# Gate and up with three pairs of seven products in the second chunk, the residual stream put away by GpSimd in halves, and both token tiles' activations transposed in one step

## The chip, the core and the metric

The kernel runs on one core of a Trainium2 chip. Five engines work side by side, each through its own queue in order: TensorE (PE, matmuls; weights are loaded in a second row, PEld), VectorE (DVE), ScalarE (ACT), GpSimd (POOL) and SyncE (SP), which here only issues transfers (DMAs). Semaphores tie the queues together. The metric is the device time of one execution in microseconds (us), the median of some runs. The profile comes from one execution of its own.

## The reference

A trunk of two layers over 256 tokens of width 2048, all in float32. Each layer, shortened:

```python
h = rms_norm(x, pre_mix_norm[l])
m = hybrid_mixer(h, ...)              # w_in, two kinds of attention, w_o
x = x + rms_norm(m, post_mix_norm[l])
h = rms_norm(x, pre_ffn_norm[l])
f = (silu(h @ w_gate[l]) * (h @ w_up[l])) @ w_down[l]     # 2048 -> 5632 -> 2048
x = x + rms_norm(f, post_ffn_norm[l])
```

The change lies in the second half of a layer, and in how x is kept while it runs.

## The kernel before

**Tokens and products.** The tokens form two tiles (t) of 128. A float32 product is made of three matmuls of a reduced type: each operand is split into `hi` (rounded) and `lo` (what is left), and hi·hi, hi·lo and lo·hi are added up in PSUM (`product`, L921 to L927). For the weights ACT makes `hi` (L250) and DVE `lo` (L252), 128 × 1024 at a time, which is one *block*: 256 rows of a weight matrix by 512 columns. `raw134` is the 134th block in the order in which all weights are loaded; `hi134` and `lo134` are its parts.

**Gate and up.** The 5632 columns are worked in 11 chunks (c) of 512, each over 8 row pairs (kp) of 256. For one kp a block of gate and one of up are needed, for both token tiles. `eight` (L1035) makes that of 8 products, 24 matmuls. `seven` (L1045) makes it of 7 products, 21 matmuls, in the manner of Strassen, which needs more of the other engines. The block of up is loaded into a tile `T`, and the first half of the block of gate is added to it by a DMA that accumulates, issued by POOL (L211). The block of gate is loaded into a tile `G`. `mixed_weights` (L216 to L238) then makes further sums and their splits: six DVE operations instead of two, four on ACT instead of two. Sums over the tokens' side (`pair_sums` L1028 and `token_sums`, the tiles `f`, `s`, `sh`, `sl`) are formed once for each kp of a layer and used by every chunk. The seven products of all such kp of a chunk share four extra banks (`p1`, `p6`, `p7`, `q5`), which `shared_part` (L959 to L966) puts together into four tiles `w` when the last is done; only then can the next use of those banks begin.

Which kp are sevens stands in constants: in chunk 0, `FIRST_SEVEN` = (4, 6), in the order `FIRST_ORDER`; in every other chunk `SEVEN` = (2, 4, 5, 6). `FORM_AT` says ahead of which step n of chunk 0 the sums of a kp are formed: 4 and 6 at steps 1 and 2, 5 at step 4, 2 at step 5.

**The stream of weights.** `weight_order` fixes one order for all blocks. `fetch` (L184) issues the loads on SP in this order, except that a `T` is asked for up to four blocks early (`EARLY`, L186 to L188). There are 4 rooms for `raw`, 6 each for `hi` and `lo`, 3 for `G` and 4 for `T`; a load waits until its room is free, that is until `hi` and `lo` of the block four `raw` earlier are made, and all loads behind it on SP wait too. `feed` (L240) issues the splits. Blocks 134 to 143 are the first of gate and up in layer 0 that matter here: 134 to 137 and 142, 143 are plain, 138 (`G`) and 139 (`T`) belong to kp 4, 140 and 141 to kp 6.

**The order of work.** The program is written as one sequence, and a planner arranges the operations of each engine, partly under `high_priority` and `manual_schedule`. Each engine's order is fixed before the kernel runs. Where an operation is issued thus decides what it may stand behind.

**x.** The residual stream x lies in four tiles `x_t_h` (token tile t, half h of 1024 columns). Two stretches of each layer have no room for it, so it is written to DRAM and loaded back: `put_away`, called after the end of the output projection (L1007) and, between the layers, after that of the down projection (L1196). The write goes out in four DMAs of 512 KB from ACT's queue (L295), as soon as `rescale` (L480 to L492), which adds the branch to x in four steps of 512 columns, and the sums of squares (`inv_rms`, L407) are issued. `rescale` takes a function `then`, called after each of the four steps: so `transposed` (L375) turns x for the next product, into the tiles `xF` (for gate and up) or `xI` (for the next layer's input projection). `transposed` is four PE transposes, four ACT copies (L383) and four DVE operations (L388). In the first stage of gate and up `G140` lies where a tile of x lay.

**The turning of activations.** At the end of a chunk silu(gate)·up is formed for both token tiles, `sg[0]` and `sg[1]`. The generator `flip` (L1084 to L1090) transposes them on PE, four transposes to a token tile, with one ACT copy (L1089) each. It is started `DEFER_ACT` = 7 ticks into the next chunk; a tick is a place between products, and each `yield 1` puts the rest off to the next.

```python
def flip(sg=sg, at=at, c=c):
    for t in range(NT):
        pb = (bank if c % 2 else acc_bank)(f"actT_ps{l}_{c}_{t}")
        for j in range(4):
            nc.tensor.transpose(pb[:, j * P : (j + 1) * P], sg[t][:, j * P : (j + 1) * P], ident)
        nc.scalar.copy(at[:, :, t * P : (t + 1) * P], pb.rearrange("p (k q) -> p k q", k=4))
        yield 1
```

Of the kernel before, what the change touches and what calls it, by code (L numbers as in the profile page):

```python
# [9 lines left out]
F32 = mybir.dt.float32  # L10
# [7 lines left out]
P = 128  # L18
# [21 lines left out]
SEVEN = (2, 4, 5, 6)  # L40
FIRST_SEVEN = (4, 6)
FIRST_ORDER = (0, 1, 3, 2, 7, 4, 6, 5)
FORM_AT = {1: 4, 2: 6, 4: 5, 5: 2}
DOWN_SEVEN = (3, 6, 9, 12, 15, 18)

WARM = 13
# [4 lines left out]

def lambda_init(layer):
    return 0.8 - 0.6 * math.exp(-0.3 * layer)


def weight_order():

    order = []

    def queue_pair(name, l, kp, c):  # L60
        order.append((name, l, kp, c))
        return len(order) - 1

    plan = []
    sevens, plain = set(), set()
    for l in range(L):
        lay = {"in": {}, "o": {}, "gate": {}, "up": {}, "down": {}}
        for n, (ca, cb) in enumerate(PAIRS):
            for kp in IN_ORDER if n else range(KT // 2):
                lay["in"][ca, kp] = queue_pair("w_in", l, kp, ca)  # L70
                lay["in"][cb, kp] = queue_pair("w_in", l, kp, cb)
                if kp in IN_NOW[n]:
                    plain.add(lay["in"][cb, kp])
        order_o = [(c, kp) for kp in KP_O for c in (0, 1)]
        order_o += [(c, kp) for c in (2, 3) for kp in range(KT // 2)]
        lay["order_o"] = order_o
        for c, kp in order_o:
            lay["o"][c, kp] = queue_pair("w_o", l, kp, c)
        for c in range(FF // CW):
            for kp in FIRST_ORDER if c == 0 else range(KT // 2):  # L80
                lay["gate"][c, kp] = queue_pair("w_gate", l, kp, c)
                lay["up"][c, kp] = queue_pair("w_up", l, kp, c)
                if kp in (FIRST_SEVEN if c == 0 else SEVEN):
                    sevens.add(lay["up"][c, kp])
        for half in range(2):
            for kp in range(FF // P // 2):
                for c in (2 * half, 2 * half + 1):
                    lay["down"][c, kp] = queue_pair("w_down", l, kp, c)
                if kp in DOWN_SEVEN:
                    sevens.add(lay["down"][2 * half + 1, kp])  # L90
        plan.append(lay)
    return order, plan, sevens, plain
# [48 lines left out]
def kernel(  # L141
# [145 lines left out]
        cols = slice(h * D // 2, (h + 1) * D // 2)  # L287
        nc.sync.dma_start(xs[t][h], xv[t][:, cols] if src is None else src[:, t, cols])

    def put_away(nm):  # L290

        away.append(kept.tile([P, NT, D], F32, name=f"away_{nm}"))
        for t in range(NT):
            for h in range(2):
                nc.scalar.dma_start(away[-1][:, t, h * D // 2 : (h + 1) * D // 2], xs[t][h])  # L295

    x_pool = [None]

    def new_x_pool(nm):
        if x_pool[0] is not None:  # L300
            x_pool[0].release()
        x_pool[0] = tc.alloc_tile_pool(name=nm, bufs=1, side="right", reuse_waits="tile")
        return x_pool[0]
# [668 lines left out]
    for l in range(L):  # L972
# [29 lines left out]
        with tc.manual_schedule(engines={mybir.EngineType.Activation, mybir.EngineType.DVE}):  # L1002
            feed(idx + 6)
            for kp in range(4, 8):
                unit(accs, mix, idx + kp - 4, kp, (0,), False, kp == 7, 0)
            evac_chunk(pool, accs[0], mg, ssm, gpost, 3, 0, f"o{l}")
            rescale(mg, ssm, 0, f"o{l}")  # L1007
            for kp in range(4, 8):
                feed(idx + 3 + kp)
                fetch(min(idx + 8 + kp, idx + 12))  # L1010
                unit(accs, mix, idx + kp - 4, kp, (1,), False, kp == 7, 0)
                transposed(0, 32 + l * KT, xT, cols=(kp - 4,))
        with tc.high_priority(offset=URGENT):
            evac_chunk(pool, accs[1], mg, ssm, gpost, 3, 1, f"o{l}")
            rescale(mg, ssm, 1, f"o{l}", lambda t, c: transposed(t, 32 + l * KT, xT, cols=(c,)))
        rs = [inv_rms(t, pool, f"ffn{l}") for t in range(NT)]
        put_away(f"ffn{l}")
        pool.release()


# [30 lines left out]

        for c in range(FF // CW):
            banks = four_banks(c % 2, [f"c{q}_{l}_{c}" for q in ("11", "12", "21", "22")])
            mine = FIRST_SEVEN if c == 0 else SEVEN
            order = FIRST_ORDER if c == 0 else tuple(range(KT // 2))
            if c == 0:
                for t in range(NT):
                    for kp in order[:2]:
                        eight(banks, c, kp, (t,), kp == order[0], False)
                order = order[2:]  # L1060
            extra = None
            for n, kp in enumerate(order):
                if c == 0 and n in FORM_AT:
                    with after_rests():
                        pair_sums(FORM_AT[n])
                if kp not in mine:
                    eight(banks, c, kp, range(NT), kp == 0, kp == order[-1])
                    continue
                if kp == mine[0]:
                    extra = four_banks(1 - c % 2, [f"{q}_{l}_{c}" for q in ("p1", "p6", "p7", "q5")])  # L1070
                seven(banks, extra, c, kp, kp == mine[0], kp == mine[-1])
                if kp == mine[-1]:
                    w = [pool.tile([P, CW], F32, tag="t2", name=f"w{j}_{l}_{c}") for j in range(4)]
                    shared_part(extra, w)
            at = pool.tile([P, 4, S], F32, tag="act", bufs=FF // CW, name=f"act{l}_{c}")
            act.append(at)
            sg = [w[0], w[2]]
            for t, u in ((0, w[1]), (1, w[3])):
                nc.vector.tensor_tensor(out=sg[t], in0=banks[2 * t], in1=sg[t], op=shared_sign(t, 0))
                nc.scalar.activation(sg[t], sg[t], AF.Silu, scale=rs[t][:, 0:1])  # L1080
                nc.vector.tensor_tensor(out=u, in0=banks[2 * t + 1], in1=u, op=ALU.add)
                nc.vector.scalar_tensor_tensor(out=sg[t], in0=u, scalar=rs[t][:, 0:1], in1=sg[t], op0=ALU.mult, op1=ALU.mult)
# [4 lines that stand above are left out]
                    for j in range(4):  # L1087
                        nc.tensor.transpose(pb[:, j * P : (j + 1) * P], sg[t][:, j * P : (j + 1) * P], ident)
                    nc.scalar.copy(at[:, :, t * P : (t + 1) * P], pb.rearrange("p (k q) -> p k q", k=4))  # L1089
                    yield 1  # L1090

            start(flip(), DEFER_ACT)
        gu.release()
# [9 lines left out]
        for half in range(2):  # L1103
# [64 lines left out]
            if half == 1:  # L1168
                xT = None
                if l + 1 < L:  # L1170
                    new_x_pool(f"x{l + 1}")
                    xT = x_tiles(f"xI{l}")
            for t in range(NT):
                if not tail:
                    for c in cc:
                        evac_sum(pool, accs[c, t], mg, ssm, gpost, c, t, f"d{l}")
                    continue
                for c in cc:
                    for kp in range(nkp - tail, nkp):
                        tick()  # L1180
                        prep(kp)
                        jh, jl = split[kp]
                        hi, lo = weights(plan[l]["down"][c, kp], LOOKAHEAD)
                        for kk in range(2):
                            sh, sl = jh[:, kk, t * P : (t + 1) * P], jl[:, kk, t * P : (t + 1) * P]
                            last = kp == nkp - 1 and kk == 1
                            nc.tensor.matmul(accs[c, t], sh, hi[:, kk, :], start=False, stop=False)
                            nc.tensor.matmul(accs[c, t], sh, lo[:, kk, :], start=False, stop=False)
                            nc.tensor.matmul(accs[c, t], sl, hi[:, kk, :], start=False, stop=last)
                    with tc.high_priority(offset=URGENT):  # L1190
                        evac_sum(pool, accs[c, t], mg, ssm, gpost, c, t, f"d{l}")
                with tc.high_priority(offset=URGENT):
                    rescale(mg, ssm, t, f"d{l}", store if xT is None else lambda t, c: transposed(t, (l + 1) * KT, xT, cols=(c,)))
        if l + 1 < L:
            rs = [inv_rms(t, pool, f"in{l + 1}") for t in range(NT)]
            put_away(f"in{l + 1}")  # L1196
        if l + 1 == L:
            x_pool[0].release()
        dn.release()
# [51 lines left out]
```

## Time and profile before

| | |
|---|---|
| median of 3 runs | 2214.32 us (2211.67 to 2216.69) |
| the profiled execution | 2215.14 us, span 2213.4 us |
| granted TensorE clock | 0.998 of full |
| matmuls and transposes | 10009 |
| transfers | 466.73 MB, mean 211 GB/s |
| gate and up | about 407 to 880 us in layer 0, 1507 to 1980 us in layer 1 |

The span runs from the first to the last instruction; 1.74 us of the profiled execution lie outside it. A row of the timeline gives the start and the duration in us, the engine, the line, the operation, the tile written and those read, and in brackets how long the engine sat idle before it and what ended that. `SPq` and `ACTq` are the sequencers that issue transfers; a row with "x3" holds three instructions in a row, and its duration includes what the queue waited between them. In the view of waits each line gives a waiting line, what it waited for, the total in us, how many times, and the longest.

### The profile page before, as it was taken

The numbers are of one execution on the slowest core, as the hardware profiler recorded it, in microseconds if no ns is written. First come the engines' busy times: TensorE is split into PE (matmuls) and PEld (weight loads), VectorE is DVE, ScalarE is ACT, GpSimd is POOL, SyncE is SP. The second block draws the span as 40 slices with busy tenths as digits, with TensorE's granted clock in tenths as the row PEclk, the third lists the DMA queues.
The fourth block names the chain that finished last, engine by engine and source line by source line (L and its number), as shares of the span: only waits on it lengthen the run. The fifth ranks groups of instructions, "written<-read, shape, count | busy, mean of one in ns | idle before, by whom it ended". The sixth has DMA issues, their size and how long they took to land.

```text
span 2213.4 us, 28454 instructions
## 1 busy us (share of the span) xinstructions
PE 2185.5 (99%) x10009; PEld 1790.9 (81%) x10009; DVE 1864.0 (84%) x2548; ACT 1354.6 (61%) x2030; POOL 142.2 (6%) x184
## 2 busy tenths in 40 slices
PE   9999999999999999999999999999999999999998
PEld 7788888778888888888888888887788888888886
DVE  7888655899999998989788886559999999999897
ACT  7566664656656656656565656646666556566564
POOL 1200000000000000000011000000000000000000
PEclk9999999999999999999999999999999999999999
DMA  8654555776776775767465545558677677667672
GB/s 304 208 180 153 190 176 186 250 237 215 218 256 211 211 258 180 241 215 240 157 239 190 177 160 177 174 187 268 208 225 235 224 221 238 226 204 243 200 254 98
DMA packets 138079, 466.73 MB, mean 211 GB/s; under 512 B 15824, under 2 KB 16336, under 8 KB 137424
## 3 DMA queue, kind: packets, MB, share of 16 engines
q1 hardware_dynamic: 120512, 430.30, 56.3%
q0 software_dynamic: 15552, 28.32, 7.5%
q10 hardware_dynamic: 1872, 6.31, 0.7%
q8 instruction: 78, 1.28, 0.2%
q14 instruction: 65, 0.53, 0.1%
HBM read 456.47 MB, written 8.39 MB: 210 GB/s over the span
## 4 chain that ended last, share of the span: by engine, by line
PE 78%; DVE 11%; DMA 4%; issue 3%; ACT 3%; SPq 0%; DVEq 0%; ACTq 0%
PE c L925 7%; PE c L926 7%; PE c L927 7%; PE in L925 5%; PE in L927 5%; PE in L926 5%; PE dn L1136 5%; PE dn L1135 5%; PE dn L1138 5%; DVE lo L252 3%; DMA raw<-in_weights_in_turn_dram 3%; PE o L464 3%; PE o L466 3%; PE o L465 3%; DVE Tl L226 2%
## 5 line engine op out<-in xcount | busy, mean ns | idle before, releaser
L252 DVE TENSOR_TENSOR lo<-raw,hi 128x1024 fp32r<-128x1024 f32 x534 | 643.3, 1223 | 161.4 <-ACT hi L250 161.2
L250 ACT ACTIVATE hi<-raw 128x1024 fp32r<-128x1024 f32 x534 | 552.4, 1053 | 235.1 <-DMA raw<-in_weights_in_turn_dram 63.5
L925 PE MATMUL c<-hi,xF 128*128 128x512 f32 x820 | 321.8, 395 | 6.2 <-DVE w L966 4.0
L926 PE MATMUL c<-lo,xF 128*128 128x512 f32 x820 | 320.0, 391 | 0.0
L927 PE MATMUL c<-hi,xF 128*128 128x512 f32 x820 | 318.3, 390 | 0.0
L211 POOL DMA_DIRECT2D T<-in_weights_in_turn_dram x108 | 94.3, 873 | 1669.3 <-PE c L926 520.9
L925 PEld LDWEIGHTS c<-hi,xF 128*128 128x128 f32 x820 | 153.7, 188 | 40.8 <-DVE w L966 6.3
L1135 PE MATMUL dn<-hi,jh 128*128 128x512 f32 x464 | 180.7, 389 | 0.0
L1136 PE MATMUL dn<-lo,jh 128*128 128x512 f32 x464 | 180.5, 389 | 0.0
L926 PEld LDWEIGHTS c<-lo,xF 128*128 128x128 f32 x820 | 154.1, 188 | 32.0 <-DVE lo L252 1.6
L927 PEld LDWEIGHTS c<-hi,xF 128*128 128x128 f32 x820 | 153.9, 188 | 32.1
L252 DVE TENSOR_TENSOR lo<-G,hi 128x1024 fp32r<-128x1024 f32 x108 | 131.7, 1220 | 26.7 <-ACT hi L250 26.6
L225 ACT ACTIVATE Th<-T 128x512 fp32r<-128x512 f32 x108 | 67.8, 627 | 138.6 <-DVE T L232 126.7
L1138 PE MATMUL dn<-hi,jl 128*128 128x512 f32 x464 | 142.9, 389 | 0.0
L226 DVE TENSOR_TENSOR lo<-T,hi 128x1024 fp32r<-128x1024 f32 x108 | 131.7, 1220 | 10.9 <-ACT hi L225 10.3
L226 DVE TENSOR_TENSOR Tl<-G,Th 128x1024 fp32r<-128x1024 f32 x108 | 131.8, 1220 | 9.6 <-ACT Th L225 9.6
L225 ACT ACTIVATE hi<-T 128x1024 fp32r<-128x1024 f32 x108 | 113.4, 1050 | 40.4 <-PE c L927 19.9
L225 ACT ACTIVATE Th<-G 128x1024 fp32r<-128x1024 f32 x108 | 113.9, 1054 | 36.6 <-DVE G L233 35.2
L233 DVE TENSOR_TENSOR G<-G,T 128x1024 f32<-128x1024 f32 x108 | 132.0, 1222 | 2.1
L925 PE MATMUL in<-hi,xT 128*128 128x512 f32 x328 | 131.5, 402 | 0.5 <-ACT hi L738 0.5
L925 PE MATMUL in<-hi,xI 128*128 128x512 f32 x328 | 131.3, 402 | 0.2 <-ACT xI L383 0.2
L926 PE MATMUL in<-lo,xT 128*128 128x512 f32 x328 | 128.2, 391 | 1.0 <-DVE lo L252 0.8
(376 smaller groups left out, 4660.2 us busy)
## 6 DMA issues: line engine op xcount, KB each, us to landing
raw<-in_weights_in_turn_dram SPq DMA_DIRECT2D x534, 512.0 KB, 4.7
T<-in_weights_in_turn_dram SPq DMA_DIRECT2D x108, 512.0 KB, 4.7
G<-in_weights_in_turn_dram SPq DMA_DIRECT2D x108, 512.0 KB, 4.8
T<-in_weights_in_turn_dram POOLq DMA_DIRECT2D x108, 256.0 KB, 6.7
GU<-in_weights_in_turn_dram SPq DMA_DIRECT2D x32, 512.0 KB, 4.6
away_ffn<-x ACTq DMA_DIRECT2D x8, 512.0 KB, 6.1
xd<-away_ffn SPq DMA_DIRECT2D x8, 512.0 KB, 9.2
xr<-in_x_columns_dram SPq DMA_DIRECT2D x8, 256.0 KB, 6.7
```

The source lines that it names most:

```text
L211: nc.gpsimd.dma_start(sums[i][:, 0, :], stream[i - 1][:, 0, :], accum_op=ALU.add)
L225: nc.scalar.activation(h, w, AF.Copy)
L226: nc.vector.tensor_tensor(out=l, in0=w, in1=h.bitcast(F32), op=ALU.subtract)
L233: nc.vector.tensor_tensor(out=g, in0=g, in1=t2.unsqueeze(1).to_broadcast([P, 2, CW]), op=ALU.add)
L250: nc.scalar.activation(hi, raw, AF.Copy)
L252: rest = nc.vector.tensor_tensor(out=lo, in0=raw, in1=hi.bitcast(F32), op=ALU.subtract)
L925: nc.tensor.matmul(a, sh, hi, start=first, stop=False)
L926: nc.tensor.matmul(a, sh, lo, start=False, stop=False)
L927: nc.tensor.matmul(a, sl, hi, start=False, stop=last)
L1135: nc.tensor.matmul(accs[c, t], sh, hi[:, kk, :], start=first, stop=False)
L1136: nc.tensor.matmul(accs[c, t], sh, lo[:, kk, :], start=False, stop=False)
L1138: nc.tensor.matmul(accs[c, t], sl, hi[:, kk, :], start=False, stop=last)
```

## The change

Three parts, in one diff.

1. In chunk 1 the seven-product pairs are kp 4, 5 and 6; kp 2 is made of eight products there, and of seven from chunk 2 on. The token sums of kp 2 are formed ahead of step 3 of chunk 1 instead of step 5 of chunk 0.
2. x is put away by GpSimd. `put_away` is called from `rescale`'s `then`, and after every second step writes the half of x that is complete with a DMA from POOL's queue. The room in DRAM is made before (`room_away`).
3. `flip` turns both token tiles in one step: its `yield 1` stands after the loop.

```diff
+NEXT_SEVEN = (4, 5, 6)
-FORM_AT = {1: 4, 2: 6, 4: 5, 5: 2}
+FORM_AT = {(0, 1): 4, (0, 2): 6, (0, 5): 5, (1, 3): 2}
...
+def gate_sevens(c):
+
+    return (FIRST_SEVEN, NEXT_SEVEN)[c] if c < 2 else SEVEN
...
-                if kp in (FIRST_SEVEN if c == 0 else SEVEN):
+                if kp in gate_sevens(c):
...
-    def put_away(nm):
-
+    def room_away(nm):
         away.append(kept.tile([P, NT, D], F32, name=f"away_{nm}"))
-        for t in range(NT):
-            for h in range(2):
-                nc.scalar.dma_start(away[-1][:, t, h * D // 2 : (h + 1) * D // 2], xs[t][h])
+
+    def put_away(t, c):
+
+        if c % 2 == 1:
+            nc.gpsimd.dma_start(away[-1][:, t, (c - 1) * CW : (c + 1) * CW], xs[t][c // 2])
...
-            rescale(mg, ssm, 0, f"o{l}")
+            room_away(f"ffn{l}")
+            rescale(mg, ssm, 0, f"o{l}", put_away)
...
-            rescale(mg, ssm, 1, f"o{l}", lambda t, c: transposed(t, 32 + l * KT, xT, cols=(c,)))
+            rescale(mg, ssm, 1, f"o{l}", lambda t, c: (transposed(t, 32 + l * KT, xT, cols=(c,)), put_away(t, c)))
         rs = [inv_rms(t, pool, f"ffn{l}") for t in range(NT)]
-        put_away(f"ffn{l}")
...
-            mine = FIRST_SEVEN if c == 0 else SEVEN
+            mine = gate_sevens(c)
...
-                if c == 0 and n in FORM_AT:
+                if (c, n) in FORM_AT:
                     with after_rests():
-                        pair_sums(FORM_AT[n])
+                        pair_sums(FORM_AT[c, n])
...
                     nc.scalar.copy(at[:, :, t * P : (t + 1) * P], pb.rearrange("p (k q) -> p k q", k=4))
-                    yield 1
+                yield 1
...
+                    room_away(f"in{l + 1}")
                     xT = x_tiles(f"xI{l}")
...
-                    rescale(mg, ssm, t, f"d{l}", store if xT is None else lambda t, c: transposed(t, (l + 1) * KT, xT, cols=(c,)))
+                    rescale(mg, ssm, t, f"d{l}", store if xT is None else lambda t, c: (transposed(t, (l + 1) * KT, xT, cols=(c,)), put_away(t, c)))
         if l + 1 < L:
             rs = [inv_rms(t, pool, f"in{l + 1}") for t in range(NT)]
-            put_away(f"in{l + 1}")
```

Counted in the built programs: PE has 6 matmuls more, DVE 8 operations fewer, ACT 4 splits and 12 DMA issues fewer, POOL 12 DMA issues more and 2 accumulating ones fewer. On SP the number of loads is the same and their order differs in places: at the start of gate and up the loads of `raw142` and `raw143` come ahead of those of `T139`, `T141` and `G138`, behind which they stood before. On ACT `hi134` to `hi136` come ahead of `xF_12` to `xF_15`.

## The prediction

> **What bounds the kernel now.** First the page's busy rows, then what PE waits for, then the stretches around those waits. TensorE (PE) is the bound nearly everywhere.
>
> ```profile
> PE 2185.5 (99%) x10009; PEld 1790.9 (81%) x10009; DVE 1864.0 (84%) x2548; ACT 1354.6 (61%) x2030; POOL 142.2 (6%) x184
> ```
>
> A matmul row lasts 0.39 us, but the rows start 0.23 us apart (461.62, 461.85, 462.08): they are pipelined, and a matmul costs 0.227 us. What can be won without taking matmuls away is only what PE stands idle. The view of PE's waits lists it:
>
> ```profile
> PE c L925 <- DVE w L966: 4.0, 2, 2.1
> PE p L925 <- ACT Th L225: 2.0, 2, 1.0
> ...
> PE p L926 <- DVE Tl L226: 1.6, 4, 0.6
> PE c L925 <- ACT hi L250: 1.6, 4, 0.6
> ...
> PE q L925 <- ACT sh L937: 0.7, 2, 0.4
> ```
>
> The columns are total us, times, longest. Every one with an even count comes once or twice in each layer, at the start of gate and up, and at the same place. I measure each by how far the start of a matmul exceeds the 0.227 us of an undisturbed one; that adds about 0.11 to the wait shown. Layer 0, with layer 1 alike: (A) 407.8 to 420.3, `xF` and `hi`, 1.9, of which 1.36 are the two `hi` waits. (B) 439 to 443, `Tl` and `lo`, 0.9. (C) chunk 1's first pair of seven products, `sh` at 461.3 and `Th` at 465.8, 1.9. (D) 496.35, `w`, 2.3. (E) five of 0.3 to 0.95 between 508 and 613, 2.1. Later chunks have none: chunk to chunk 41.7 us (671.24 to 713.02 to 754.73), in which DVE is busy 39.1 of 41.8. So DVE has 2.7 us of slack in a steady chunk, and a delay at the start takes several chunks to work off: C, D and E are that.
>
> D, in the timeline of DVE and the chain of waits (start, duration, what):
>
> ```profile
> 490.44 0.68 DVE L964 TENSOR_TENSOR w<-p,w 128x512 f32<-128x512 f32 x1
> 493.87 1.23 DVE L252 TENSOR_TENSOR lo<-raw,hi 128x1024 fp32r<-128x1024 f32 x1 [2.74 <-ACT hi L250]
> 495.01 0.68 DVE L965 TENSOR_TENSOR w<-q,w 128x512 f32<-128x512 f32 x1
> 495.61 0.68 DVE L966 TENSOR_TENSOR w<-q,w 128x512 f32<-128x512 f32 x1
> ```
>
> ```profile
> 485.37 7.33 DMA raw<-in_weights_in_turn_dram
> ```
>
> A `lo` of a weight block whose load was only issued at 485.37 stands ahead of L965 and L966 on DVE, and PE needs the bank that L966 frees.
>
> The last thing to read is the first mixed block of gate and up, `T139`. It is loaded by SP, added to by POOL, and then split on ACT:
>
> ```profile
> 408.58 0.86 SPq L210 DMA_DIRECT2D T<-in_weights_in_turn_dram  x2
> 409.54 11.56 SPq L195 DMA_DIRECT2D G<-in_weights_in_turn_dram  x2
> 421.19 2.03 SPq L202 DMA_DIRECT2D raw<-in_weights_in_turn_dram  x3
> ```
>
> ```profile
> SPq L195 <- DMA away_ffn<-x: 10.7, 1, 10.7
> ```
>
> ```profile
> 414.22 1.01 POOL L211 DMA_DIRECT2D T<-in_weights_in_turn_dram  x1 [260.46 <-PE c L926]
> 416.75 0.87 POOL L211 DMA_DIRECT2D T<-in_weights_in_turn_dram  x1 [1.52 <-ACT xF L383]
> ```
>
> ```profile
> 413.35 1.14 ACT L383 ACTIVATE xF<-xT_ps,gains 128x128 fp32r<-128x128 f32 x4 [1.35 <-PE xT_ps L380]
> ...
> 418.30 3.89 ACT L250 ACTIVATE hi<-raw 128x1024 fp32r<-128x1024 f32 x4
> ...
> 427.26 1.04 ACT L225 ACTIVATE hi<-T 128x1024 fp32r<-128x1024 f32 x1
> ```
>
> SP loads `T139` at 408.58 (landed 413.56); POOL's addition goes out at 414.22 and lands 5.45 us later, at 419.67. ACT reads the block only at 427.26, so it has 7.6 us to spare. SP stands 10.7 us for x's write, since G140 lies where x lay. PE's first matmul with `Th139` is at 434.08.
>
> **The change, part by part.**
>
> Products. Each layer gets three more matmuls: 3 × 0.227 = +0.7 us. One pair of blocks fewer is mixed: DVE loses two operations of 1.14 and two of 0.60 us (pitches in the DVE timeline) = 3.5 us, ACT two, POOL one addition. DVE is not the bound in steady chunks, so the 3.5 us are worth only what they take from C, D and E. Chunk 1's first pair of seven is now kp 4 instead of kp 2: two more plain pairs stand before it (24 matmuls, 5.4 us each), against a lateness of 1.9. C goes: −1.9 (ends −1.9 and −1.0, if `sh` or `Th` of kp 4 is still late). D: in the changed program L965 and L966 stand ahead of that `lo`, behind the one before it, whose load may still be 0 to 1.5 us late: 0.5 is left, −1.8 (ends −2.3 and −0.8). E: five small waits for DVE, which now has 3.5 us less to do; I leave 0.7 of 2.1, −1.4 (ends −2.1 and 0). B stays at 0.9.
>
> x put away. Twelve 512 KB writes go from ACT's queue to POOL's. On ACT an issue lasts 0.33 us and lies beside other work: nothing. On POOL an issue lasts 0.87 to 1.01 us; the four of a place stand before the additions for `T139` and `T141`. The last half of x is ready at 414.4 by the row of before; POOL is free by 415.5, before the additions now come. SP no longer stands for 10.7 us. But the order of the queues moves with it, and this is the dear part: on SP the loads `raw142` and `raw143` (gate and up of kp 5) now stand *ahead* of `T139`, `T141`, `G138`. `raw143` takes `raw135`'s room and so waits for `lo135`. On ACT `hi134` to `hi136` move ahead of `xF_12` to `xF_15`: from 414.4, where `xF_11`'s row ends, at a pitch of 0.95, `hi135` ends at 416.4, and on DVE `lo134` and `lo135` (1.14 and 1.22, with a few small rows between) end near 418.0. So `T139` is issued at 418.4 instead of 408.58. It lands 4.98 us later (as before), 423.4; POOL issues at 423.5; the addition lands 5.45 us later in layer 0 (its row) and 6.8 in layer 1 (both rows there, 6.6 and 7.0): L = 429.0 and 430.3 on layer 0's clock, 429.7 on average. Ends: 428 (4.4 for the load, the least among the `T` rows of this stretch, and 5.0 for the addition) and 432 (the page's median of 6.7 for the addition, and 6.5 for a load behind others).
>
> From `hi139` to PE's first matmul with `Th139` ACT's queue takes 434.08 − 427.26 = 6.8, of which it idled 0.28: 6.5. That matmul comes at L + 6.5 = 436.2, against 434.08: **+2.1**. The 1.36 of `hi` waits in A do go, since `hi134` to `hi136` come earlier, but PE only reaches the wait for `Th139` so much sooner: nothing is left of it. DVE's `lo139`, 428.53 before, comes at L + 1.1 = 430.8, 2.3 late like PE, so B isn't changed.
>
> In the Trainium skill, "DMA: Bandwidth & Descriptors", section "Issuing engines are not separate DMA queues", transfers from all issuing engines share the same 16 DMA engines, so that another issuer saves only issue time. By it this part alone would be worth the ACT issues, 4 × 0.33 us a place, which lie beside other work: nothing. The row of SP's 10.7 us agrees: what counts there is where the write stands in order, not who carries it.
>
> Put-away between the layers: the four writes leave ACT, POOL is idle there, and a few `hi` move by under 1 us: 0 ± 1, in the sum once.
>
> Flip. Two groups of four transposes become one of eight. From PE's rows, a group of eight costs 0.88 (879.33 to 880.12 and the late start after it), one of four 0.44 each: a saving of about 0.02 in each of 20 chunks, −0.4. Both copies (L1089) then come together on ACT, which is at 61%.
>
> Sum per layer: +0.7 − 1.9 − 1.8 − 1.4 + 2.1 = −2.3. Two layers −4.6, flip −0.4: −5.0. The profiled execution took 2215.14 (span 2213.4 and 1.74 around it), 0.8 above the median of 2214.32. 2215.1 − 5.0 = 2210.1 on its clock, **2209** beside the median. With the ends of L alone (−1.7 and +2.3 in each layer) 2206 to 2214.
>
> **The rivals.** A change of under 0.2% (4.4 us) can hardly be told from none here.
>
> *T isn't late.* If `T139` lands by 427.3, say because `raw143`'s room is free earlier, the first matmul is no later, and A's 1.36 counts too: per layer +0.7 − 1.9 − 1.8 − 1.4 − 1.3 = −5.7, in all −11.8: 2203. For it: 7.6 us of slack before. Against: it needs 2.4 us less than the rows add up to.
>
> *The waits move one chunk on.* DVE's steady slack is 2.7 us a chunk and its sums for kp 2 are now formed inside chunk 1; the late load of D and the small waits of E return in chunk 2, where four pairs of seven begin again at kp 2. Then only C is won: +0.7 − 1.9 + 2.1 = +0.9 a layer, +1.8 − 0.4 in all: 2216. For it: E shows that a delay is carried through three chunks. Against: 3.5 us of DVE's work really go.
>
> *The software queue is the bound (slower).* POOL's queue carries the four writes of x and then the additions. 512 KB transfers land 1.26 us apart in a burst, so if an addition waits for four of them, L is 5.0 later: 434.7 instead of 429.7, and 2 × 5.0 − 5.0 = +5.0: 2219. It decides from L = 432.2 (no gain) and costs 2 us for each us of L; from 434.4 on it is over 0.2%. For it: the additions, 256 KB each, already take 6.7 us to land against 4.7 for SP's 512 KB. Against: the last write is issued some 8 us before the first addition, longer than the 6.1 us that such writes took to land from ACT's queue. On the same page, section "SWDGE vs HWDGE vs iDMA", the Trainium skill says that only one software queue is allocated, and that GpSimd writes its descriptors itself. No row here shows writes and additions queued together; by that rule the later arrival is this rival.
>
> **How the numbers follow.** Forecast 0.48 (0.30 of it below −4.4 us, the rest within, as L runs from 428 to 432), T not late 0.16 (faster), waits moved on 0.14 (same) and 0.02 beyond it, software queue 0.20 (slower). Faster 0.30 + 0.16 = 0.46; same 0.18 + 0.14 = 0.32; slower 0.22. The range takes in the first rival and the third, 2203 to 2219.5; what lies past either end, some 15%, is left out.
>
> **What would show it.** Right: on SP two `raw` loads between x's last and `T139`, `hi<-T` on ACT near 430 with ACT and DVE idle some 5 us before it; PE's list without `sh` L937 and `Th` L225 for kp 2, but with a new wait for `Th` or `hi<-T` near 434; `w` L966 under 0.6; SP without the 10.7 us; 176 transposes in groups of eight. Wrong: `hi<-T` near 427 (first rival), waits between 508 and 540 as large as those that went (second), an addition that lands over 9 us after its issue (third).

## The result and the profile after

The changed kernel is slower by 0.56%: 2226.62 us, median of 4 runs (2224.61 to 2228.21), beside 2214.08 before; the ratio is 1.0056, 95% interval 1.0039 to 1.0073. The profiled execution took 2224.61 us, span 2222.9, which is 9.5 above the span of before; that is what the traces have to explain. (The medians are 12.5 apart: the profiled execution was the fastest of the four.)

Where it went is read best between four places that both traces have: the first transpose of x at the end of the output projection, the first matmul with `Th139` (and its like in layer 1), and the first matmul of layer 1's input projection on `xI`. Start to start, in us:

| | before | after | |
|---|---|---|---|
| span's start to the end of output projection, layer 0 | 396.21 | 395.41 | −0.8 |
| from there to the first mixed product | 37.87 | 44.10 | **+6.2** |
| to layer 1's input projection | 671.42 | 667.70 | −3.7 |
| to the end of layer 1's output projection | 390.49 | 392.07 | +1.6 |
| to layer 1's first mixed product | 37.86 | 44.18 | **+6.3** |
| to the end | 679.55 | 679.44 | −0.1 |

So the loss lies in two equal stretches, one per layer, and what the chunks win back pays for a part of it in layer 0 and for none in layer 1. The short stretches are safe: they are 37.8 to 37.9 in the kernel before and in the three variants below that leave x's writes and SP's order alone. The long ones are less so: the first, in which no part of the change lies, goes from 394.6 to 397.6 over all the kernels below, and the third is 671.4 before and 669.5 with the flip alone, which is worth nothing that can be measured.

In the stretch, SP and POOL first (timeline of the changed kernel):

```profile
398.46 18.97 SPq L208 DMA_DIRECT2D raw<-in_weights_in_turn_dram  x6
417.48 0.90 SPq L216 DMA_DIRECT2D T<-in_weights_in_turn_dram  x2
...
414.65 0.53 POOL L302 DMA_DIRECT2D away_ffn<-x  x1 [7.70 <-DVE ssx_ffn L417]
424.69 0.91 POOL L217 DMA_DIRECT2D T<-in_weights_in_turn_dram  x1 [9.51 <-DMA T<-in_weights_in_turn_dram]
...
432.38 1.06 ACT L231 ACTIVATE hi<-T 128x1024 fp32r<-128x1024 f32 x1 [4.75 <-DMA T<-in_weights_in_turn_dram]
```

Six `raw` loads take SP 19 us, since the last of them stand for rooms; `T139` goes out at 417.48 where it went out at 408.58. POOL, free since 415.2, stands 9.5 us until it has landed, and ACT 4.75 us for POOL's addition. Then PE (timeline):

```profile
429.99 0.40 PE L934 MATMUL c<-hi,xF 128*128 128x512 f32 x1
433.49 0.49 PE L932 MATMUL q<-hi,sh 128*128 128x512 f32 x1 [3.10 <-ACT hi L231]
434.75 0.68 PE L933 MATMUL q<-lo,sh 128*128 128x512 f32 x1 [0.77 <-DVE lo L232]
435.22 0.63 PE L934 MATMUL q<-hi,sl 128*128 128x512 f32 x1
435.65 0.63 PE L932 MATMUL c<-hi,sh 128*128 128x512 f32 x1
...
439.51 0.73 PE L932 MATMUL p<-Th,sh 128*128 128x512 f32 x2 [0.45 <-ACT Th L231]
440.08 0.40 PE L933 MATMUL p<-Tl,sh 128*128 128x512 f32 x1
```

PE stands 3.1 us for `hi<-T`. After that a second thing shows that no row of the kernel before has in gate and up: the matmul rows last 0.63 instead of 0.39 us and start 0.43 apart instead of 0.23. The table by stretches gives the granted clock beside it (stretch, its length, PE's busy time, granted clock, DMA share, GB/s):

```profile
435.00:438.00 3.00, 2.98 (x7) 0.50 0.62 117
...
1118.00:1121.00 3.00, 3.00 (x10) 0.50 0.97 266
...
1538.00:1544.00 6.00, 4.99 (x10) 0.50 0.85 200
1544.00:1548.00 4.00, 4.00 (x11) 0.54 0.68 244
```

The clock is half after the stall in each layer, and once more at 1118, after two waits of 1.1 and 0.5 us at layer 1's start. In layer 0 it is full again when `Th139` comes; in layer 1 it lasts until 1547.5, 4 us past the first mixed product.

The waits that the first part was to take away are partly gone. PE's waits over the whole execution:

```profile
PE q L932 <- ACT hi L231: 6.6, 2, 3.5
PE c L932 <- DVE w L973: 2.9, 3, 1.2
PE p L933 <- DVE Tl L232: 2.4, 6, 0.6
...
PE xT_ps L387 <- DVE rsq_d_p L378: 1.1, 1, 1.1
```

`sh` for kp 2 has gone; `w` went from 4.0 to 2.9; `Tl` rose from 1.6 to 2.4; and the first line is new and larger than all of them. The last line lies at the start of layer 1's input projection; before, it was

```profile
PE xT_ps L380 <- DVE rsq_d_p L371: 0.3, 1, 0.3
```

### The profile page after: what moved, and what is told of

Its sections match the earlier page's. It is cut to its first block, busy times and chain, and to the rows that moved or that the text cites. A ratio compares the mean times of both kernels' runs of the same rounds, so it can differ in the third digit from the quotient of the medians.

```text
span 2222.9 us, 28470 instructions
## 1 busy us (share of the span) xinstructions
PE 2191.5 (99%) x10015; PEld 1798.3 (81%) x10015; DVE 1853.5 (83%) x2540; ACT 1351.1 (61%) x2026; POOL 144.7 (7%) x194
## 4 chain that ended last, share of the span: by engine, by line
PE 86%; DVE 6%; ACT 3%; DMA 3%; issue 2%; SPq 0%; DVEq 0%; POOL 0%; ACTq 0%; POOLq 0%
PE c L932 8%; PE c L933 8%; PE c L934 8%; PE in L932 6%; PE in L934 6%; PE in L933 6%; PE dn L1142 5%; PE dn L1143 5%; PE dn L1145 5%; PE o L471 3%; PE o L473 3%; PE o L472 3%; PE p L933 2%; PE p L932 2%; PE p L934 2%
## 5 line engine op out<-in xcount | busy, mean ns | idle before, releaser
L932 PE MATMUL c<-hi,xF 128*128 128x512 f32 x834 | 327.2, 393 | 4.7 <-DVE w L973 2.9
L933 PE MATMUL c<-lo,xF 128*128 128x512 f32 x834 | 325.0, 390 | 0.0
L934 PE MATMUL c<-hi,xF 128*128 128x512 f32 x834 | 324.8, 391 | 0.0
L932 PEld LDWEIGHTS c<-hi,xF 128*128 128x128 f32 x834 | 157.0, 188 | 40.3 <-DVE w L973 4.7
L934 PEld LDWEIGHTS c<-hi,xF 128*128 128x128 f32 x834 | 156.7, 188 | 32.5
L256 ACT ACTIVATE hi<-G 128x1024 fp32r<-128x1024 f32 x106 | 111.6, 1053 | 35.9 <-issue 23.6
```

The source lines that it names most:

```text
L256: nc.scalar.activation(hi, raw, AF.Copy)
L932: nc.tensor.matmul(a, sh, hi, start=first, stop=False)
L933: nc.tensor.matmul(a, sh, lo, start=False, stop=False)
L934: nc.tensor.matmul(a, sl, hi, start=False, stop=last)
```

## The experiments

Theory O: the order on SP, with `raw142` and `raw143` ahead of `T139`, is the whole of it. Theory Q: POOL's queue is slow, because x's writes and the additions share it. Theory P: three pairs in chunk 1 cost more than they bring. Each ratio is against the kernel before, run on the same chip in between.

**The order mended.** Everything as in the changed kernel, only that two loads may not overtake `T141`:

```diff
+    behind = {lay[m][0, 5]: lay["up"][0, 6] for lay in plan for m in ("gate", "up")}
...
+            if i in behind:
+                with tc.issue_after(t_loads[behind[i]].ins):
+                    loads.append(nc.sync.dma_start(raw, stream[i]))
```

> The changed kernel, with one thing mended: on SP the loads of raw142 and raw143 (and their like in layer 1) are issued behind those of T139 and T141, as in the kernel before. Theory O (the order on SP makes T139 late): its load goes out near 408.6 again and not at 417.5, its addition lands by 421 and not at 432.4, PE's idle of 3.1 and 3.5 us ahead of the first mixed product goes, and the half clock after it. Per layer some 6 us come back and 2 us more in layer 1, some of it taken by what is late next: 2211 to 2216. Theory Q (POOL's software queue is slow, because x's writes and the additions share it): the addition still takes 7.7 us or more from its issue, and the time stays at 2223 or more.

Measured: 2208.84, ratio 0.9976 (0.9967 to 0.9985). The loss is gone and a gain stands in its place. Its timeline, SP, POOL and ACT:

```profile
408.63 1.39 SPq L222 DMA_DIRECT2D T<-in_weights_in_turn_dram  x2
...
415.57 0.53 POOL L309 DMA_DIRECT2D away_ffn<-x  x1 [7.68 <-DVE ssx_ffn L424]
416.15 1.85 POOL L224 DMA_DIRECT2D T<-in_weights_in_turn_dram  x2
...
425.11 1.05 ACT L238 ACTIVATE hi<-T 128x1024 fp32r<-128x1024 f32 x1
```

`T139` goes out as early as before, the additions go out right behind x's last write, and ACT reads the block in its turn without a wait. The stretch to the first mixed product is 36.62 in both layers, 1.25 below that of before: the two `hi` waits, which the changed order on ACT takes away. What theory Q foresaw for the time doesn't come: the same writes on the same queue do no harm. Its first sign does come: the additions for `T139` took 8.3 us in layer 0 and 8.0 in layer 1, more than the 7.7 named for it, against 6.0 and 6.4 with the same writes on ACT's queue (below). The first landed at 424.4, not by 421, and 0.7 us before ACT read the block. So they are slow behind the writes, and issued this early it just suffices. Whether it is the queue or the loads beside them that makes them slow, no run separates. The time lies under the range, which had let the next wait eat a part of what was freed; what is late next is small.

**Without the second part.** Parts one and three on the kernel before.

> The changed kernel without its second part: x is put away from ACT's queue as before; three pairs of seven in chunk 1 and the flip in one step stay. Theory O: SP's order is that of before, so T139 is on time; C goes, D and E shrink: 2.4 us a layer as between the two traces, and 0.4 for the flip: 2209, 2206 to 2212. Theory P (the three pairs in chunk 1 cost more than they bring, whatever the order): 2216 or more.

Measured: 2211.37, ratio 0.9988 (0.9979 to 0.9997). Theory P falls. The stretch to the first mixed product is 37.81 and 37.83, that of before.

**The second part alone.**

> The kernel before with the second part alone: x put away by GpSimd in halves. Theory O: T139 is late by some 6 us in each layer, with half a clock after it and 2.5 us between the layers, and no gain in the chunks: 2226 to 2232. Theory P: 2212 to 2216.

Measured: 2228.84, ratio 1.0067 (1.0054 to 1.0080). The stretch is 43.88 and 43.89, SP has the same order as in the changed kernel. So it is this part that moves the loads, alone and without the others. The two stretches hold 12.1 of its loss of 15.2.

**The writes between the layers back on ACT.**

```diff
-                    rescale(mg, ssm, t, f"d{l}", store if xT is None else lambda t, c: (transposed(t, (l + 1) * KT, xT, cols=(c,)), put_away(t, c)))
+                    rescale(mg, ssm, t, f"d{l}", store if xT is None else lambda t, c: transposed(t, (l + 1) * KT, xT, cols=(c,)))
         if l + 1 < L:
             rs = [inv_rms(t, pool, f"in{l + 1}") for t in range(NT)]
+            for t in range(NT):
+                for h in range(2):
+                    nc.scalar.dma_start(away[-1][:, t, h * D // 2 : (h + 1) * D // 2], xs[t][h])
```

> The changed kernel with the writes of x between the layers back on ACT's queue, behind the sums of squares, as before; those within a layer stay with GpSimd. If the wait for rsq_d_p at the start of layer 1 (1.1 us and a stretch at half clock) comes from part two there, 2.5 us come back: 2224. If it is only a shift of what was before, 2226 to 2227.

Measured: 2222.63, ratio 1.0034 (1.0022 to 1.0046). The two profiled spans are only 2.5 apart (2220.4 and 2222.9). The stretch from layer 1's input projection to the end of its output projection is 390.11 instead of 392.07 in them, 2.0 less, so what was expected is there in these two traces (the two runs with small matmuls below, which leave this place as the changed kernel has it, have 391.1 and 391.5). That the medians are 4.0 apart is more than it explains, and the intervals of the two ratios overlap.

**The order alone, on the kernel before.** `raw142` and `raw143` are loaded ahead of `T139` and `T141`; ACT still writes x, chunk 1 has four pairs.

```diff
+    late = {lay["gate"][0, 4]: (lay["gate"][0, 5], lay["up"][0, 5]) for lay in plan}
+    not_before = {lay["up"][0, kp]: lay["gate"][0, 4] for lay in plan for kp in FIRST_SEVEN}
...
+            if i in late:
+                for k in late[i]:
+                    ahead[k] = wpool.tile([P, 2, CW], F32, tag="raw", bufs=4, name=f"raw{k}")
+                    loads.append(nc.sync.dma_start(ahead[k], stream[k]))
...
-                if j in sevens and j not in sums:
-                    summed(j)
+                if j in sevens and j not in sums and i >= not_before.get(j, 0):
+                    with tc.issue_after(loads[-1].ins):
+                        summed(j)
```

> The kernel before with one thing changed: on SP the loads of T139 and T141 (and their like in layer 1) stand behind raw142 and raw143; x is still put away from ACT's queue, four pairs of seven in chunk 1. Theory O (the order on SP alone is the cost): raw143 waits for lo135, which ends at 421.7 there, so T139 goes out near 422, its addition lands at 433 to 437, PE stands some 3 us or more ahead of the first mixed product in each layer: 2226 to 2236. Theory W (GpSimd's writes of x are needed for it): 2212 to 2218.

Measured: 2224.76, ratio 1.0047 (1.0033 to 1.0060), a little under the range. The timeline:

```profile
419.92 1.47 SPq L190 DMA_DIRECT2D raw<-in_weights_in_turn_dram  x2
421.44 0.90 SPq L221 DMA_DIRECT2D T<-in_weights_in_turn_dram  x2
...
437.88 1.06 ACT L236 ACTIVATE hi<-T 128x1024 fp32r<-128x1024 f32 x1 [9.05 <-DMA T<-in_weights_in_turn_dram]
```

The late load alone makes the kernel slower, without a write from GpSimd. The edit does a little more than the order on SP, since the additions stand inside it too: in layer 0 `T139` landed at 427.15, and POOL issued its addition only 5.5 us later, by the trace for a matmul of PE:

```profile
432.67 2.81 POOL L222 DMA_DIRECT2D T<-in_weights_in_turn_dram  x3 [279.57 <-PE c L938]
```

In layer 1 it followed the landing by 0.7 us, and the lateness is as large there, so this isn't what makes it. The run also tells the price of lateness: the first mixed product comes 12.8 and 13.0 us later than before, but the whole is only 10.7 longer. Between that place and the next landmarks 7 to 8 us come back in each layer (663.54 instead of 671.42, and 672.62 instead of 679.55): while PE stands, ACT and DVE split blocks ahead, as far as rooms allow, and the waits D and E of the kernel before don't come (C does, at 469.8 and 474.6). D and E were 4.4 a layer; where the other 3 come from isn't shown.

**Small matmuls in the wait.** To price the half clock, 40 matmuls of 128 columns on constants were put where PE stands, into a bank that is overwritten from zero afterwards:

```diff
+            if n == 2:
+                for _ in range(warm):
+                    nc.tensor.matmul(p7[:, 0:P], ident16, hidden, start=True, stop=True)
             product(*job)
```

> The changed kernel with 40 small matmuls (128 columns, constants, overwritten before use) ahead of the first q product in each layer, where PE stands for 3.1 and 3.5 us. Theory H (after the idle stretch the granted clock is halved, and that costs time of its own): matmuls stay 0.23 us apart after it; in layer 1, where half the clock lasted 3.5 us beyond the first mixed product, 2 us come back, in layer 0 little: 2223 to 2225.5. If the half clock lies wholly beside the wait for Th, or the small matmuls take longer than the wait: 2226 to 2229.

Measured: 2226.72, ratio 1.0053 (1.0040 to 1.0066). It settles nothing: the planner set the q products together, PE then stood 4.0 and 4.8 us for `Th` behind them, and the half clock came after that wait instead.

**Small matmuls in both waits.** 40 more ahead of the product with `Th`, into the bank p6.

> As the run with 40 small matmuls, and 40 more behind the q product, where PE then stood for 4.0 and 4.8 us waiting for Th; the wait itself stays. Theory H: the granted clock is no longer halved after it; in the run before, the matmuls after that wait stood 0.427 us apart, 12 in layer 0 and 10 in layer 1, 0.2 us each too many, so up to 4.8 us come back against 2226.7: 2221 to 2224, unless the waits that come next (Tl, w) take up a part. If the half clock lies beside waits that end later anyway: 2225 or more.

Measured: 2220.92, ratio 1.0034 (1.0022 to 1.0046). PE's timeline in layer 1:

```profile
1539.85 2.41 PE L969 MATMUL p<-hidden,ident 128*128 128x128 bf16 x40
1543.99 0.49 PE L932 MATMUL p<-Th,sh 128*128 128x512 f32 x1 [1.73 <-ACT Th L231]
...
1546.04 0.40 PE L934 MATMUL p<-Th,sl 128*128 128x512 f32 x1
1546.27 0.39 PE L932 MATMUL p<-Th,sh 128*128 128x512 f32 x1
```

The block comes no sooner, yet the matmuls behind it are 0.23 apart. In layer 0 the small matmuls did not keep the clock: after waits of 1.1 and 0.75 us it was halved all the same, and the second 40 took 3.6 us instead of 2.4:

```profile
438.85 3.63 PE L969 MATMUL p<-hidden,ident 128*128 128x128 bf16 x40
```

There the half clock fell on them and was over at 441.4, before the first mixed product at 442.5. By the ratios the run is 0.19% or 4.2 us below the one with the first 40 alone. The two intervals overlap a little, so the size is not sure, but the traces carry it: in the former run 12 matmuls in layer 0, 10 in layer 1 and 8 more in chunk 2 stood 0.43 apart, at 0.2 each some 6 us, and in this one none do behind the first mixed products.

**The same points, ACT's queue.**

```diff
-            nc.gpsimd.dma_start(away[-1][:, t, (c - 1) * CW : (c + 1) * CW], xs[t][c // 2])
+            nc.scalar.dma_start(away[-1][:, t, (c - 1) * CW : (c + 1) * CW], xs[t][c // 2])
```

> The changed kernel with x put away at the same points, per token half, but from ACT's queue. Its SP order has T139 and T141 ahead of raw142 and raw143. If it is the order that decides and not who issues the writes: as the mended kernel, 2207 to 2211. If GpSimd's queue bears a cost of its own in the mended kernel: 2 us or more below that, 2206 or less; if the issues on ACT cost time among its splits: 2212 or more.

Measured: 2213.26, ratio 0.9994 (0.9985 to 1.0003); SP's order is that of before. What it gives away to the mended kernel is a wait on ACT, whose queue now holds a write that needs x:

```profile
ACT hi L256 <- DVE x L497: 4.0, 1, 4.0
```

This is a line of ACT's waits between 390 and 425. The two `hi` waits of PE go here too, but PE stands about as long for `xF` instead, and its stretch to the first mixed product is 37.81, 1.2 more than in the mended kernel, or 2.4 us in two layers. POOL has nothing else to do there. That the second part is worth about as much, once the order is mended, is seen without this run too: the mended kernel is 2.5 us below the one without part two (2208.84 and 2211.37), though their intervals overlap. The profiled execution was the fastest of this kernel's runs (2209.99) and its span equals that of the mended kernel, so what else lies between the two medians (0.18% by the ratios, 4 us) can't be seen in it and stays open.

**One part at a time.** The first part alone, the third alone:

> The kernel before with the first part alone: three pairs of seven in chunk 1. Beside the run without part two (2211.4), this tells the flip's share. If the flip brings 0.05 us a chunk, as the traces have it, 2212.4; if the flip brings nothing, 2211.4; if it brings most of the 2.2 us, 2213 or more.

> The kernel before with the third part alone: both token tiles turned in one step. From the traces 0.05 us a chunk, in 20 chunks 1.0: 2213 beside 2214. If the pairing gives back its saving elsewhere: 2214. A loss of more than 1 us (2215 or more) would mean that DVE or ACT stand for the second copy.

Measured: 2211.76, ratio 0.9989 (0.9981 to 0.9998), and 2213.28, ratio 1.0002 (0.9992 to 1.0011). The flip can't be told from nothing. The three parts alone are worth −2.3, +15.2 and +0.5, in all +13.4; together they measured +12.5.

**The mended order, and ACT between the layers.** Both edits from above.

> The mended kernel (T139 and T141 ahead on SP), and the writes of x between the layers back on ACT's queue as before. In the mended kernel's trace PE's waits at the start of layer 1 are 0.27 us longer for rsq_d_p and 0.23 for lo than before; with that undone 0.5 to 1 us below the mended kernel's 2208.8: 2207.8 to 2208.3. If part two costs nothing between the layers: 2208.8. In no case more than 2210.

Measured: 2206.60, ratio 0.9971 (0.9959 to 0.9982), the best of all, and 1.2 under the range. The intervals of the two mended kernels overlap, so that it beats the other is not shown; in the traces the stretch from layer 1's input projection to the end of its output projection is 390.41 instead of 391.21, 0.8 less, as expected.

## Why the prediction was wrong

It forecast 5 us less; 12.5 more were measured. In the profiled spans that is 14.5 us between forecast and trace. By the stretches of the first table they are 8.4 up to the first mixed products, 1.6 between the layers, 0.9 and 4.5 behind the first mixed products (−3.7 and −0.1 where −4.6 each was forecast), less the 0.8 by which the trace was ahead before the change begins.

*T139's lateness, 8.4 of them.* The order on SP, raw143's wait for `lo135`, ACT's and POOL's queues were foreseen, and the place. The size was not. The step that failed was "That matmul comes at L + 6.5 = 436.2, against 434.08: **+2.1**", and it measured +6.2 and +6.3. Its start was right: `T139` was issued at 417.5 in a trace that is 0.8 ahead at this place, so at 418.3 on the clock of before, where 418.4 was forecast. Every term behind it was too small. In layer 0 the load landed after 6.6 us instead of 4.98; POOL issued 0.6 later instead of 0.1, as it had before (413.56 to 414.22); the addition took 7.6 instead of 5.45; ACT's way from `hi139` to the first matmul with `Th139` took 7.1 instead of 6.5. In layer 1 the load took 6.1 and the addition 8.2, forecast at 6.8. On the clock of before, L was 433.2, past the upper end of 432, and the first mixed product came at 440.3, not 436.2. Both transfers were priced by the best row at hand: in the same trace the load of `T141`, issued 0.4 us behind that of `T139`, took 7.2. Here `T139` goes out in a crowd, as the table by stretches shows:

```profile
408.50:413.60 5.10, 5.10 (x26) 1.00 0.40 127
...
417.50:424.70 7.20, 7.20 (x33) 1.00 0.93 365
424.70:432.40 7.70, 5.69 (x25) 1.00 1.03 346
```

While SP stands, the DMA engines are 40% busy (84% over the same times before); when it goes on, nine loads are issued in 7 us, and the engines are full until L. That the crowd made the transfers slow is likely for the load, which took 5.3 us in both layers of the mended kernel, but not shown; the additions took 8.3 and 8.0 there too, so lateness can't be the whole reason for their length.

*The half clock, some 3.5.* It was not in the sum at all. In the trace, 2.0 in layer 1 (eight matmuls at 0.2 and one at 0.36 behind the first mixed product) are a part of the 4.5 above, and about 1.5 at layer 1's start a part of what was lost between the layers. The Trainium skill, "TensorE: Matmul & The Clock Gate", section "What's actually happening", says that the clock of the array is halved after an idle window of some 3.4 us, and is full again after as long a busy one; its section "Wait — 56ns, not 53.3ns?" gives 426.7 ns from start to start for cold matmuls of 512 columns. The spacing agrees (0.43 here), and so does the length of two of the cold stretches (434.9 to 438.3 and 1117.6 to 1121.0; the third lasted 10.2 us). The condition agrees less: waits of 0.8 and 0.8 us, 1.3 us apart, were enough at 1620 in the first run with small matmuls, and one of 1.9 at 502.8 with part two alone, while a single one of 2.1 at 496 in the kernel before was not.

*The gains of the chunks.* C went as forecast. D was to keep 0.5 and kept 1.5 in layer 0 (497.4 and 499.2), E was to keep 0.7 and kept 1.3; in layer 1 chunk 0's end has a new wait of 1.4 (`w`, 1563.3). Alone, the first part brought 2.3 us in both layers together, where the prediction had 4.4 in each. When PE's order moves up, it can meet the next block of DVE's work: in the run without part two, PE stands 1.3 us for a `lo` at 459.9, which no trace of before has.

*Between the layers, 1.6.* Forecast 0 ± 1. In ACT's queue two sums of squares now stand ahead of `rsq_d_p`, where there was one. PE waits 1.1 for it where it waited 0.3, and then runs at half clock. In four other kernels with this order on ACT, the mended one, that with part two alone and the two with small matmuls, that wait is 0.6 and the clock stays full. So 0.3 more is what the change does there; why it was 1.1 in the profiled execution of the changed kernel stays open.

*The flip.* Forecast −0.4, measured +0.5 with an interval of about ±2: no more than that it is small.

The rivals. "T isn't late" gave 2203. The mended kernel is that case made true, and took 2208.8: it won less, since D and E stay in part, and a wait of 1.2 us for a `lo` is new (460.4). "The waits move one chunk on" was right for a part of D and E. "The software queue is the bound" had the right sign and nearly the right point: it was to decide from L = 432.2, and L was 433.2 on the same clock. But it isn't what made L late here: x's last write had landed at 418.1, 6.6 us before the first addition was issued. In the mended kernel, where the additions do stand right behind the writes, they are slow (8.3 and 8.0 us) and still land in time. By its formula of 2 us for each us of L that point would have been a loss of 2; what made more of it is that the formula took the gains of the chunks as safe, and left out the clock and the longer way on ACT. The Trainium skill, "DMA: Bandwidth & Descriptors", section "SWDGE vs HWDGE vs iDMA", has only one software queue allocated; in the changed kernel that decided nothing: POOL's issues of x's writes lasted 0.53 to 0.75 us, and they landed in 3.5 us.

## What to carry to other kernels

When an edit frees a queue's wait, look at the order of that queue afterwards: what moves ahead may need a room, and everything behind it, late or not, waits too. One ordering edge on SP turned +0.56% into −0.24%. A transfer that is delayed should be priced by its delay and then by a row from a crowded moment, not by the best row of a quiet one; and a wait of several us on TensorE is longer than it looks, since what comes after it may run at half clock.

## What the runs showed of the hardware

Away from the two ends of the span, the granted clock fell to 0.50 in or behind waits of 1.9 to 7.3 us and also behind pairs of about 1 us, for 3.4, 6.8 or 10.2 us by the clock records, in the traces of all the kernels with a late `T139`, and in neither of the mended ones at these places. Matmuls of 128 columns on constants, 0.06 us each at full clock, went with a full clock through layer 1's waits in one run, and not through layer 0's in the same run. Writes of 512 KB from GpSimd took 0.53 to 0.75 us to issue, less than its accumulating transfers of 256 KB (0.87 to 0.92), and landed sooner than the same writes had from ACT's queue; the changed kernel's page, columns as before:

```profile
T<-in_weights_in_turn_dram POOLq DMA_DIRECT2D x106, 256.0 KB, 6.7
...
away_ffn<-x POOLq DMA_DIRECT2D x8, 512.0 KB, 3.5
```

They go out earlier there, in a quieter moment, which may be all of the difference.
